# Batched 64 x 64 matmul: two rows of `a` per partition, packed 64 x 32 products, and all transfers on one queue

## The chip, the cores and the metric

The kernel runs on 1 core of one Trainium2 chip. The metric is the device time of the core in microseconds (us), the median over several executions. Each experiment was timed beside the kernel before on the same chip; that kernel's median lay between 188.4 and 189.0 us in every round, so times of different rounds are compared here as they stand. A run more than 1.5% above the fastest of its kernel is called slow; ratios below use fast runs only.

Abbreviations of the profile: PE is TensorE's matmul, PEld its weight load, DVE is VectorE, ACT is ScalarE, POOL is GpSimd, SP is SyncE. `L106` is a line of the kernel. A "group" below is 64 of the 1,024 products, the unit that the kernel loads, computes and stores; there are 16.

## The reference

```python
a = randn(1024, 64, 64)   # float32
b = randn(1024, 64, 64)   # float32
out = np.matmul(a, b)     # float32
```

The inputs are 33.5 MB together, the output 16.8 MB. The kernel computes in bf16: the loads cast from fp32 on the way.

## The kernel before

For each group, four loads on GpSimd's queue bring `a` and `b`. `a` is laid out as block diagonals of two matrices, whose zeros are written once. PE transposes each block, DVE copies the result out of PSUM, PE multiplies, and DVE and ACT each copy half of the product into `o_sb`. One store for each group goes out on SyncE's queue.

```python
a_v = a.rearrange("(g p h) r n -> g h r p n", p=P2_LG, h=2)   # runs of one row: 64 fp32 = 256 B
b_v = b.rearrange("(g s h) r n -> g h r s n", s=P2_LG, h=2)
...
for lg in range(n_lg):
    a_sb = a_tiles[lg % A_BUFS]
    for h in range(2):
        nc.gpsimd.dma_start(out=a_sb[64*h : 64*h+64, :, 64*h : 64*h+64], in_=a_v[lg, h])
    b_sb = lg_pool.tile([128, P2_LG, 64], bf16, name="b_sb")
    for s0 in range(0, P2_LG, P2_LG // 2):
        nc.gpsimd.dma_start(out=b_sb[:, s0 : s0 + P2_LG//2, :], in_=b_v[lg, :, :, s0 : s0 + P2_LG//2, :])
    o_sb = lg_pool.tile([128, LG // 4, 128], out_dt, name="o_sb")
    ...  # 4 chunks: 8 transposes of 128 x 128, copy, 16 products (K=128, M=64, N=64), 2 copies
    o_dst = out[i0 : i0 + LG].rearrange("(q b4) (t u) c -> b4 t q u c", b4=4, u=2)  # runs of 512 B
    nc.sync.dma_start(out=o_dst, in_=o_sb[:, :, :])
```

## Time and profile before

| | before |
|---|---|
| time | 188.67 us (6 runs, 188.19 to 189.46) |
| PE busy | 48% of the span |
| load packets, each writing 128 B | 131,072 |
| store packets, each 512 B | 32,768 |

From the profile page of the kernel before: PE's busy time and share, the DMA engines' busy share in 40 slices of the span (9 is 90% or more), the two queues (packets, MB, and their packets' time as a share of 16 engines' span), and the chain that ended last, by engine.

```profile
...
PE 90.0 (48%) x1536; PEld 75.9 (40%) x1536; DVE 74.4 (40%) x131; ACT 24.9 (13%) x65; POOL 72.4 (39%) x70
...
DMA  5999999999999999999999999999999999999927
...
q0 software_dynamic: 132096, 16.78, 139.5%
q1 hardware_dynamic: 33024, 16.78, 42.1%
...
DMA 68%; PE 12%; issue 7%; POOL 7%; DVE 2%; ACT 0%; POOLq 0%
```

The DMA engines are busy in every slice but the first and the last two, while PE is busy half of the time. The chain is 68% DMA. GpSimd's queue (`q0`) has a share of 139.5% because one engine has several packets under way at once, 2.45 on average from 10 to 20 us (below); such a share tells overlap, not speed.

Three stretches of the kernel before (the windows view). After the length of the stretch come busy times of the engines with their instruction counts, then the granted PE clock, the DMA share (how many packets an engine has under way on average) and the GB/s written.

```profile
...
core 0: us, PE busy (x) PEld busy (x) DVE busy (x) ACT busy (x) POOL busy (x), PEclk, DMA share, GB/s
10.00:20.00 10.00, 9.04 (x168) 7.78 (x170) 6.65 (x13) 1.61 (x5) 8.25 (x8) 1.00 2.45 156
24.00:27.50 3.50, 0.39 (x4) 0.12 (x2) 1.06 (x2) 0.00 (x0) 0.29 (x1) 0.50 1.47 213
184.00:186.00 2.00, 0.00 (x0) 0.00 (x0) 0.00 (x0) 0.00 (x0) 0.00 (x0) 0.51 1.01 290
```

The three rows are the three regimes: loads alone at 156 GB/s, loads and stores mixed at 213, stores alone at 290. Since a load writes bf16 but reads fp32, 156 GB/s written is 312 GB/s read. Divided over 16 engines, a load packet of 128 B takes 13.1 ns and a store packet of 512 B takes 28.2 ns.

What PE waited for in the kernel before (total us, times, longest):

```profile
...
PE t_ps L89 <- DMA a_diag<-in_a_dram: 60.6, 15, 10.7
...
PE o_ps L102 <- DMA b_sb<-in_b_dram: 26.4, 15, 3.9
```

PE waits for data, 60.6 + 26.4 = 87.0 us.

### The profile page before, as it was taken

How to read it: one execution, taken by the hardware profiler on the slowest of the kernel's cores; microseconds unless marked ns; L12 is line 12 of the kernel's file. 1: busy time of each engine (PE TensorE's matmuls, PEld its weight loads, DVE VectorE, ACT ScalarE, POOL GpSimd, SP SyncE). 2: the span in 40 equal slices, each digit the busy share in tenths (PEclk: the TensorE clock that was granted, in tenths of full speed). 3: DMA queues.
4: the chain of work that ended last, by engine and by line, in shares of the span. 5: the costliest groups of instructions: out<-in, count | busy, mean ns of one | idle time of the engine just before them, and what ended most of it. 6: DMA issues, size and time to landing. Idle time of an engine off the chain costs nothing.

```text
span 187.6 us, 3567 instructions
## 1 busy us (share of the span) xinstructions
PE 90.0 (48%) x1536; PEld 75.9 (40%) x1536; DVE 74.4 (40%) x131; ACT 24.9 (13%) x65; POOL 72.4 (39%) x70
## 2 busy tenths in 40 slices
PE   0079516274362913558037490575603955245840
PEld 0068415264342713546036370564503744234730
DVE  6437524135061532247124360263502545035440
ACT  2002301102011110111101120020300212002020
POOL 7997512262424514265042642336222472200000
PEclk9999955557576675576756758555855587558576
DMA  5999999999999999999999999999999999999927
GB/s 37 131 155 156 174 213 212 176 176 210 163 213 168 177 211 186 200 158 187 201 195 192 156 207 180 207 181 157 212 183 213 166 158 210 184 212 167 247 65 206
DMA packets 165136, 33.79 MB, mean 180 GB/s; under 512 B 132352, under 2 KB 165120, under 8 KB 165120
## 3 DMA queue, kind: packets, MB, share of 16 engines
q0 software_dynamic: 132096, 16.78, 139.5%
q1 hardware_dynamic: 33024, 16.78, 42.1%
q8 instruction: 12, 0.20, 0.4%
q14 instruction: 4, 0.03, 0.0%
HBM read 33.55 MB, written 16.78 MB: 268 GB/s over the span
## 4 chain that ended last, share of the span: by engine, by line
DMA 68%; PE 12%; issue 7%; POOL 7%; DVE 2%; ACT 0%; POOLq 0%
DMA b_sb<-in_b_dram 57%; DMA a_diag<-in_a_dram 11%; PE t_ps L89 8%; PE o_ps L102 5%; POOL a_diag L70 4%; POOL b_sb L77 3%; DVE a_diag L60 1%; DVE t_sb L93 0%; DVE o_sb L112 0%; ACT o_sb L113 0%; POOLq L70 0%; POOLq L77 0%
## 5 line engine op out<-in xcount | busy, mean ns | idle before, releaser
L89 PE MATMUL t_ps<-identity,a_diag 128*128 128x128 bf16 x512 | 57.6, 292 | 60.6 <-DMA a_diag<-in_a_dram 60.6
L89 PEld LDWEIGHTS <-a_diag 128*128 128x128 bf16 x512 | 46.2, 133 | 63.8 <-issue 61.8
L93 DVE COPY t_sb<-t_ps 128x1024 bf16<-128x1024 bf16 x64 | 43.6, 690 | 69.6 <-PE t_ps L89 69.3
L77 POOL DMA_DIRECT2D b_sb<-in_b_dram x32 | 37.1, 1164 | 58.3 <-issue 25.5
L102 PE MATMUL o_ps<-b_sb,t_sb 128*64 128x64 bf16 x1024 | 36.6, 231 | 30.1 <-DMA b_sb<-in_b_dram 26.4
L70 POOL DMA_DIRECT2D a_diag<-in_a_dram x32 | 34.8, 1090 | 30.1 <-DMA b_sb<-in_b_dram 21.7
L102 PEld LDWEIGHTS <-t_sb 128*64 128x64 bf16 x1024 | 29.7, 142 | 40.9 <-issue 25.5
L113 ACT COPY o_sb<-o_ps 128x256 f32<-128x256 f32 x64 | 23.7, 372 | 156.0 <-DVE o_sb L112 155.8
L112 DVE COPY o_sb<-o_ps 128x256 f32<-128x256 f32 x64 | 26.7, 423 | 35.2 <-PE o_ps L102 34.1
L60 DVE MEMSET a_diag<- 128x2048 uint32 x3 | 5.3, 1765 | 2.0 <-PEq L136 1.2
L113 ACT ACT_TABLE_LOAD x1 | 1.3, 1283 | 0.7 <-PEq L136 0.7
masks.py:199 POOL TENSOR_SCALAR_AFFINE_SELECT identity<-identity 128x128 bf16<-128x128 bf16 x1 | 0.3, 307 | 0.1
masks.py:197 POOL MEMSET identity<- 128x128 bf16 x1 | 0.2, 205 | 0.3 <-POOLq L136 0.3
L136 POOL MEMSET const-float32-0.0<- 128x1 f32 x1 | 0.1, 99 | 0.2 <-issue 0.2
L136 POOL MEMSET const-uint8-127<- 128x1 uint8 x1 | 0.1, 103 | 0.0
L136 POOL MEMSET const-bfloat16-1.0<- 128x1 bf16 x1 | 0.1, 102 | 0.0
L136 POOL MEMSET const-float32-1.0<- 128x1 f32 x1 | 0.1, 99 | 0.0
## 6 DMA issues: line engine op xcount, KB each, us to landing
out_dram<-o_sb SPq DMA_DIRECT2D x16, 1024.0 KB, 11.5
b_sb<-in_b_dram POOLq DMA_DIRECT2D x32, 256.0 KB, 18.8
a_diag<-in_a_dram POOLq DMA_DIRECT2D x32, 256.0 KB, 20.4
```

Source lines behind the costliest of these rows:

```text
L60: nc.vector.memset(a_diag, 0.0)
L70: nc.gpsimd.dma_start(out=a_sb[64 * h : 64 * h + 64, :, 64 * h : 64 * h + 64], in_=a_v[lg, h],)
L77: nc.gpsimd.dma_start(out=b_sb[:, s0 : s0 + P2_LG // 2, :], in_=b_v[lg, :, :, s0 : s0 + P2_LG // 2, :],)
L89: nc.tensor.transpose(t_ps[:, pp, :], a_sb[:, p0 + pp, :], identity)
L93: nc.vector.tensor_copy(t_sb[:], t_ps[:])
L102: nc.tensor.matmul(o_ps[orows, sigma, 64 * j : 64 * j + 64], stat[:, :, j::2], b_sb[:, p, :], start=True, stop=True,)
L112: nc.vector.tensor_copy(dst[:, :half, :], o_ps[:, :half, :])
L113: nc.scalar.copy(dst[:, half:, :], o_ps[:, half:, :])
L136: nc = _bacc.Bacc("TRN2", target_bir_lowering=False, num_devices=1)
```

## The change

It does several things at once: it reads `a` in runs of two rows (512 B); it drops the block diagonals and packs products of 64 x 32 into separate tiles of the PE array; it works in chunks of 32 products instead of 16; it issues loads two groups ahead in the program; and it moves the stores from SyncE's queue to GpSimd's. The diff, cut to its core:

```diff
-    CG = 16
+    CG = 32
-    PSUM_BUFS = 3
+    PSUM_BUFS = 2
-    a_v = a.rearrange("(g p h) r n -> g h r p n", p=P2_LG, h=2)
-    b_v = b.rearrange("(g s h) r n -> g h r s n", s=P2_LG, h=2)
+    a_v = a.rearrange("(g Qi beta) (q j) k -> g beta q Qi j k", Qi=QUADS_LG, beta=4, j=2)
+    b_v = b.rearrange("(g gamma s) r n -> g gamma r s n", gamma=2, s=LG // 2)
-    ...  # three block-diagonal tiles for a, zeroed once
+    def load(lg):
+        a_sb = lg_pool.tile([128, QUADS_LG, 128], bf16, name="a_sb")
+        nc.gpsimd.dma_start(out=a_sb[:, :, :], in_=a_v[lg])
+        b_sb = lg_pool.tile([128, 4 * SLOTS_B, 64], bf16, name="b_sb")
+        for gamma in range(2):
+            rows = slice(64 * gamma, 64 * gamma + 64)
+            nc.gpsimd.dma_start(out=b_sb[rows, :, :], in_=b_v[lg, gamma])
+        loaded[lg] = (a_sb, b_sb)
+    load(0)
+    load(1)
     for lg in range(n_lg):
+        if lg + 2 < n_lg:
+            load(lg + 2)
...      # per group: 32 transposes (64 x 128) instead of 32 (128 x 128),
...      # 128 products (K=64, M=32, N=64) instead of 64 (K=128, M=64, N=64)
-            nc.sync.dma_start(out=o_dst, in_=o_sb[:, :, :])
+        nc.gpsimd.dma_start(out=o_dst, in_=o_sb[:, :, :])
```

More of the change, by code (lines that the diff above doesn't have):

```diff
@@ L28 @@
     LG = 64 if B % 64 == 0 else B
-    CG = 16
-    STORE_BF16 = False
-    A_BUFS = 3
+    CG = 32
     SBUF_BUFS = 3
-    PSUM_BUFS = 3
+    PSUM_BUFS = 2
     assert B % LG == 0 and LG % CG == 0
@@ L37 @@
     n_cg = LG // CG
-    P2_LG = LG // 2
-    P2_CG = CG // 2
-    S4_CG = CG // 4
-    a_v = a.rearrange("(g p h) r n -> g h r p n", p=P2_LG, h=2)
-    b_v = b.rearrange("(g s h) r n -> g h r s n", s=P2_LG, h=2)
+    QUADS_LG = LG // 4
+    QUADS_CG = CG // 4
+    PAIRS_CG = CG // 8
+    SLOTS_B = LG // 8
+    assert QUADS_CG % 2 == 0, "chunk must contain whole quad pairs"
+    a_v = a.rearrange(
+        "(g Qi beta) (q j) k -> g beta q Qi j k", Qi=QUADS_LG, beta=4, j=2
+    )
+    b_v = b.rearrange("(g gamma s) r n -> g gamma r s n", gamma=2, s=LG // 2)
     consts = ctx.enter_context(tc.tile_pool(name="consts", bufs=1))
-    a_pool = ctx.enter_context(tc.tile_pool(name="a_pool", bufs=1))
     lg_pool = ctx.enter_context(tc.tile_pool(name="lg", bufs=SBUF_BUFS))
@@ L55 @@
     make_identity(nc, identity)
-    a_tiles = []
-    for ai in range(A_BUFS):
-        a_diag = a_pool.tile([128, P2_LG, 128], bf16, name=f"a_diag_{ai}")
-        nc.vector.memset(a_diag, 0.0)
-        a_tiles.append(a_diag)
-    out_dt = bf16 if STORE_BF16 else fp32
+    loaded = {}
+    def load(lg):
[6 more added lines that the diff above has]
+        loaded[lg] = (a_sb, b_sb)
@@ L65 @@
+    load(0)
+    load(1)
     for lg in range(n_lg):
         i0 = lg * LG
-        a_sb = a_tiles[lg % A_BUFS]
-        for h in range(2):
-            nc.gpsimd.dma_start(
-                out=a_sb[64 * h : 64 * h + 64, :, 64 * h : 64 * h + 64],
-                in_=a_v[lg, h],
-            )
-        b_sb = lg_pool.tile([128, P2_LG, 64], bf16, name="b_sb")
-        for s0 in range(0, P2_LG, P2_LG // 2):
-            nc.gpsimd.dma_start(
-                out=b_sb[:, s0 : s0 + P2_LG // 2, :],
-                in_=b_v[lg, :, :, s0 : s0 + P2_LG // 2, :],
-            )
@@ L82 @@
-        o_sb = lg_pool.tile([128, LG // 4, 128], out_dt, name="o_sb")
-        for cg in range(n_cg):
-            p0 = cg * P2_CG
-            t_ps = ps_pool.tile([128, P2_CG, 128], bf16, name="t_ps")
-            for pp in range(P2_CG):
-                nc.tensor.transpose(
-                    t_ps[:, pp, :], a_sb[:, p0 + pp, :], identity
-                )
-            t_sb = cg_pool.tile([128, P2_CG, 128], bf16, name="t_sb")
-            nc.vector.tensor_copy(t_sb[:], t_ps[:])
-            o_ps = ps_pool.tile([128, S4_CG, 128], fp32, name="o_ps")
-            for pp in range(P2_CG):
-                p = p0 + pp
-                sigma, colp = pp // 2, pp % 2
-                orows = slice(64 * colp, 64 * colp + 64)
-                stat = t_sb[:, pp, :].rearrange("k (hh mm) -> k hh mm", hh=2)
-                for j in range(2):
-                    nc.tensor.matmul(
-                        o_ps[orows, sigma, 64 * j : 64 * j + 64],
-                        stat[:, :, j::2],
-                        b_sb[:, p, :],
-                        start=True,
-                        stop=True,
-                    )
-            half = S4_CG // 2
-            dst = o_sb[:, cg * S4_CG : (cg + 1) * S4_CG, :]
-            nc.vector.tensor_copy(dst[:, :half, :], o_ps[:, :half, :])
-            nc.scalar.copy(dst[:, half:, :], o_ps[:, half:, :])
@@ new lines @@
+        if lg + 2 < n_lg:
+            load(lg + 2)
+        a_sb, b_sb = loaded.pop(lg)
+        o_sb = lg_pool.tile([128, QUADS_LG, 128], fp32, name="o_sb")
+        for cg in range(n_cg):
+            t_ps = ps_pool.tile([128, PAIRS_CG, 2, 128], bf16, name="t_ps")
+            for w in range(PAIRS_CG):
+                for gamma in range(2):
+                    Qi = QUADS_LG // 2 * gamma + cg * PAIRS_CG + w
+                    trows = slice(64 * gamma, 64 * gamma + 64)
+                    for j in range(2):
+                        nc.tensor.transpose(
+                            t_ps[trows, w, j, :],
+                            a_sb[:, Qi, 64 * j : 64 * j + 64],
+                            identity,
+                        )
+            t_sb = cg_pool.tile([128, PAIRS_CG, 2, 128], bf16, name="t_sb")
+            nc.vector.tensor_copy(t_sb[:], t_ps[:])
+            o_ps = ps_pool.tile([128, QUADS_CG, 128], fp32, name="o_ps")
+            for j in range(2):
+                for ql in range(QUADS_CG):
+                    w, gamma = ql // 2, ql % 2
+                    wl = cg * PAIRS_CG + w
+                    slot = (QUADS_CG // 2) * gamma + w
+                    rows = slice(64 * gamma, 64 * gamma + 64)
+                    for beta in range(4):
+                        nc.tensor.matmul(
+                            o_ps[
+                                32 * beta : 32 * beta + 32,
+                                slot,
+                                64 * j : 64 * j + 64,
+                            ],
+                            t_sb[rows, w, j, 32 * beta : 32 * beta + 32],
+                            b_sb[rows, 4 * wl + beta, :],
+                            start=True,
+                            stop=True,
+                            tile_position=(64 * gamma, 32 * beta),
+                        )
+            half = QUADS_CG // 2
+            lo = cg * PAIRS_CG
+            hi = QUADS_LG // 2 + lo
+            nc.vector.tensor_copy(o_sb[:, lo : lo + half, :], o_ps[:, :half, :])
+            nc.scalar.copy(o_sb[:, hi : hi + half, :], o_ps[:, half:, :])
@@ L115 @@
         o_dst = out[i0 : i0 + LG].rearrange(
-            "(q b4) (t u) c -> b4 t q u c", b4=4, u=2
+            "(Qi b4) (t u) c -> b4 t Qi u c", b4=4, u=2
         )
-        if STORE_BF16:
-            nc.gpsimd.dma_start(out=o_dst, in_=o_sb[:, :, :])
-        else:
-            nc.sync.dma_start(out=o_dst, in_=o_sb[:, :, :])
+        nc.gpsimd.dma_start(out=o_dst, in_=o_sb[:, :, :])
 _INS = ['a', 'b']
```

## The prediction

> **What bounds the kernel now.** The 16 DMA engines. The page's slices show DMA at 9 tenths in nearly all of the 187.6 us span, PE only 48% busy. The chain that ended last is 68% DMA, most of it `b_sb<-in_b_dram` (57%). PE waits for data (waits: `a_diag` 60.6 us, `b_sb` 26.4 us). Windows show three DMA regimes: loads alone 156 GB/s (10 to 20 us), stores alone 290 GB/s (184 to 186 us), both together 213 GB/s (24 to 27.5 us). The loads are 131,072 packets that write 128 B each (fp32 256 B read, bf16 written), the stores 32,768 packets of 512 B. Per engine, a load packet takes 128 B x 16 / 156 GB/s = 13.1 ns, a store packet 512 B x 16 / 290 GB/s = 28.2 ns. Loads alone would need 107 us, stores 58 us, together 165 us. The DMA is busy from about 3 to 187 us less a 3 us gap near 181 us, so mixing the two queues costs some 15 us more.
>
> **What the change does.** Time bought on PE, DVE or ACT is worth nothing here.
> 1. `a` is loaded in runs of two rows: 32,768 packets of 512 B read and 256 B written, instead of 65,536. `b` keeps its 65,536, the stores their 32,768. Bytes do not change. [...]
> 2. Stores move from SyncE's queue to GpSimd's, which carries the loads. Transfers then run one after another instead of interleaving. I expect most of the 15 us of mixing to go.
> 3. The diagonal zero fill (5.3 us DVE) goes; loads start no earlier.
> 4. PE: 512 transposes of half the columns, and 2,048 small matmuls instead of 1,024. At the trace's 36 ns per small matmul (16 in 0.57 us) and about 85 ns per transpose (estimate, below today's full-width 117 ns), a group of 64 products costs 7 to 8 us of PE against about 10 us of DMA. It stays hidden. DVE copies fall from 70 to about 45 us.
> 5. GpSimd still issues 64 DMAs: four per group at 1.1 us, hidden. A store waiting in this queue blocks later loads, but two groups are loaded ahead, so the DMA should not run dry.
>
> **Sum.** 53.7 (`b`) [...] + 57.8 (stores) = 157.5 us, plus 3 us before the first packet and 2 to 3 us at the end: about 163 us. Range 149 to 178. Chances: faster by over 2% 0.93, within 2% 0.04, slower 0.03.
>
> **What would show it.** DMA still at 9 tenths in all slices; about 131,000 packets, all on the software queue; [...] stores alone at about 290; no long stretch at 213. PE above 60% busy, its waits still for `a_sb` and `b_sb`.
>
> **What would make it wrong.** If a 512 B read costs two 256 B reads (26 ns), 170 us or more. If packets cost the same whatever their size, below 150 us. If software-queue stores do not take 28 ns, 10 us either way. If small matmuls cost over 50 ns, PE becomes the bound; gaps in the DMA slices would show it, as would a store that starves the loads.

The forecast's sum came to 157.5 us, and with the start and the end to about 163 us. Two terms are 4,096 x 13.1 ns for `b` and 2,048 x 28.2 ns for the stores, both from the trace before. The 85 ns for a transpose are the author's estimate; with them, products of 50 ns would make 32 x 85 + 128 x 50 ns = 9.1 us of PE for a group, beside about 10 us of DMA (estimate).

## The result, and the profile after

| | before | after |
|---|---|---|
| time | 188.79 us (16 runs, 188.19 to 189.46) | 155.04 us (8 runs, 154.93 to 155.49) |
| ratio to before | | 0.8217, 95% interval 0.8202 to 0.8233 |

A ratio is the mean time of one kernel's fast runs over that of the other's fast runs of the same rounds, so it is not quite the ratio of the medians. The kernel is 17.8% faster, inside the predicted range and 8 us below its centre.

From the profile page of the changed kernel, the same parts as above, with the count of packets and the queue that brings instructions (`q8`):

```profile
...
PE 58.6 (38%) x2560; PEld 48.4 (32%) x2560; DVE 43.4 (28%) x64; ACT 20.0 (13%) x33; POOL 72.7 (47%) x70
...
DMA  1999999999999999999999999999999999999955
...
DMA packets 103446, 33.90 MB, mean 221 GB/s; under 512 B 99328, under 2 KB 99328, under 8 KB 103424
...
q0 software_dynamic: 103424, 33.56, 171.0%
q8 instruction: 20, 0.33, 0.8%
...
issue 37%; POOL 34%; DMA 21%; PE 3%; POOLq 1%
```

The DMA engines are still busy throughout, except at the very start and end, and PE is busy even less. There are 103,446 packets, not the predicted 131,000. The missing ones are stores: 103,424 - 99,328 = 4,096 packets lie between 2 and 8 KB, and the record of single packets gives each of them 4,096 B, where SyncE's queue moved 32,768 of 512 B. So GpSimd's queue joined eight runs into one packet. "issue" in the chain is time for which the profile names no wait.

Waits of the changed kernel:

```profile
...
PE t_ps L90 <- DMA a_sb<-in_a_dram: 50.7, 15, 7.5
...
POOL out_dram L128 <- ACT o_sb L123: 21.9, 5, 8.2
...
PE o_ps L106 <- issue: 16.9, 8, 4.2
...
PE o_ps L106 <- DMA b_sb<-in_b_dram: 7.0, 14, 1.3
```

PE still waits for data, 50.7 us for `a` (60.6 before) and 7.0 us for `b` (26.4 before). Two rows are new. PE waits 16.9 us for "issue", a wait whose cause this view does not name; it matters below. And GpSimd waits 21.9 us for products before it can issue a store, with later loads standing behind that store in its queue.

The pace of the steady state is read from the chain of the changed kernel in order of time (start, length in us, what). Each row is the issue of one group's store:

```profile
...
94.39 1.17 POOL out_dram L128
...
103.23 1.17 POOL out_dram L128
...
112.39 1.17 POOL out_dram L128
...
121.67 1.17 POOL out_dram L128
...
130.98 1.17 POOL out_dram L128
```

Four groups take 130.98 - 94.39 = 36.6 us, so one takes 9.15 us, against the predicted 157.5 / 16 = 9.84 us.

PE's part of one group, from the timeline of the changed kernel (start, length, line, count, idle time before it):

```profile
...
84.75 1.92 PE L90 MATMUL t_ps<-identity,a_sb 128*64 128x128 bf16 x32 [4.32 <-DMA a_sb<-in_a_dram]
...
88.08 1.24 PE L106 MATMUL o_ps<-b_sb,t_sb 64*32 64x64 bf16 x120 [0.38 <-DMA b_sb<-in_b_dram]
```

A transpose takes 1.92 / 32 = 60 ns and a small product 1.24 / 120 = 10.3 ns.

Two windows near the end of the changed kernel, both of stores alone (columns as before):

```profile
...
core 0: us, PE busy (x) PEld busy (x) DVE busy (x) ACT busy (x) POOL busy (x), PEclk, DMA share, GB/s
142.00:146.00 4.00, 1.56 (x128) 1.20 (x124) 1.95 (x3) 1.01 (x2) 0.00 (x0) 1.00 1.00 315
149.00:152.00 3.00, 0.00 (x0) 0.00 (x0) 0.00 (x0) 0.00 (x0) 0.00 (x0) 1.00 0.99 287
```

Between these, from 146.5 to 148 us, the DMA engines have almost nothing to do (a DMA share of 0.14, 52 GB/s): the last store had to wait for the last products.

### The profile page after: what moved, and what is told of

The parts are those of the page before. It is cut to its first block, busy times and chain, and to the rows that moved or that the text cites. A ratio compares the mean times of both kernels' runs of the same rounds, so it can differ in the third digit from the quotient of the medians.

```text
span 153.7 us, 5443 instructions
## 1 busy us (share of the span) xinstructions
PE 58.6 (38%) x2560; PEld 48.4 (32%) x2560; DVE 43.4 (28%) x64; ACT 20.0 (13%) x33; POOL 72.7 (47%) x70
## 2 busy tenths in 40 slices
DMA packets 103446, 33.90 MB, mean 221 GB/s; under 512 B 99328, under 2 KB 99328, under 8 KB 103424
## 3 DMA queue, kind: packets, MB, share of 16 engines
q0 software_dynamic: 103424, 33.56, 171.0%
## 4 chain that ended last, share of the span: by engine, by line
issue 37%; POOL 34%; DMA 21%; PE 3%; POOLq 1%
DMA a_sb<-in_a_dram 21%; POOL b_sb L68 17%; POOL a_sb L63 9%; POOL out_dram L128 8%; PE t_ps L90 3%; POOLq L154 1%; POOL identity masks.py:199 0%; POOL identity masks.py:197 0%; POOLq L128 0%; POOLq L63 0%; POOLq L68 0%; POOLq masks.py:199 0%; POOLq L143 0%
## 5 line engine op out<-in xcount | busy, mean ns | idle before, releaser
L90 PE MATMUL t_ps<-identity,a_sb 128*64 128x128 bf16 x512 | 31.1, 314 | 52.9 <-DMA a_sb<-in_a_dram 50.7
L68 POOL DMA_DIRECT2D b_sb<-in_b_dram x32 | 34.9, 1095 | 28.1 <-DMA out_dram<-o_sb 21.1
L90 PEld LDWEIGHTS <-a_sb 128*64 128x64 bf16 x512 | 27.0, 173 | 55.1 <-DMA a_sb<-in_a_dram 52.6
L106 PE MATMUL o_ps<-b_sb,t_sb 64*32 64x64 bf16 x2048 | 28.5, 231 | 33.1 <-issue 16.9
L96 DVE COPY t_sb<-t_ps 128x1024 bf16<-128x1024 bf16 x32 | 22.1, 692 | 61.2 <-PE t_ps L90 61.2
L128 POOL DMA_DIRECT2D out_dram<-o_sb x16 | 18.8, 1173 | 40.4 <-ACT o_sb L123 21.9
L123 ACT COPY o_sb<-o_ps 128x512 f32<-128x512 f32 x32 | 18.8, 586 | 125.4 <-DVE o_sb L122 125.3
L106 PEld LDWEIGHTS <-t_sb 64*32 64x32 bf16 x2048 | 21.4, 101 | 41.0 <-issue 26.2
L122 DVE COPY o_sb<-o_ps 128x512 f32<-128x512 f32 x32 | 21.3, 689 | 41.0 <-PE o_ps L106 41.0
L63 POOL DMA_DIRECT2D a_sb<-in_a_dram x16 | 18.6, 1163 | 5.9 <-DMA b_sb<-in_b_dram 2.8
```

The source lines that it names most:

```text
L63: nc.gpsimd.dma_start(out=a_sb[:, :, :], in_=a_v[lg])
L68: nc.gpsimd.dma_start(out=b_sb[rows, :, :], in_=b_v[lg, gamma])
L90: nc.tensor.transpose(t_ps[trows, w, j, :], a_sb[:, Qi, 64 * j : 64 * j + 64], identity,)
L96: nc.vector.tensor_copy(t_sb[:], t_ps[:])
L106: nc.tensor.matmul(o_ps[32 * beta : 32 * beta + 32, slot, 64 * j : 64 * j + 64,], t_sb[rows, w, j, 32 * beta : 32 * beta + 32], b_sb[rows, ...
L122: nc.vector.tensor_copy(o_sb[:, lo : lo + half, :], o_ps[:, :half, :])
```

## The experiments

Four things could explain the gain: the shared queue, the larger reads of `a`, the look-ahead, and the lighter PE work. The main theory was that transfers alone set the time and that the queue brings most of it. The rivals are named in each expectation.

### 1. Undo the queue

```diff
-        nc.gpsimd.dma_start(out=o_dst, in_=o_sb[:, :, :])
+        nc.sync.dma_start(out=o_dst, in_=o_sb[:, :, :])
```

> The changed kernel with one thing undone: the stores go back to SyncE's queue, in 512 B packets, a is still read in 512 B runs. Theory (the shared queue ends the mixing of loads and stores, which cost about 15 us): 165 to 170 us, with long windows of one mixed rate, near 220 GB/s. Rival (the gain of 34 us comes from a's larger reads, or from the smaller PE work, and not from the queue): within 2% of 155 us.

Measured: 181.21 us, ratio 0.9609 to the kernel before. With the stores back on SyncE's queue, 26 of the 34 us are lost. A window of this run:

```profile
...
core 0: us, PE busy (x) PEld busy (x) DVE busy (x) ACT busy (x) POOL busy (x), PEclk, DMA share, GB/s
60.00:63.00 3.00, 0.29 (x8) 0.17 (x9) 0.69 (x1) 0.00 (x0) 1.09 (x1) 1.00 1.45 213
```

The mixed regime of 213 GB/s is back. The rival (`a`'s reads or PE bring the whole gain) is refuted. This run keeps the loads two groups ahead, so it shows what the queue is worth beside the look-ahead. The theory's size was also too small: the loss was larger than the 10 to 15 us expected.

### 2. Undo the larger reads of `a`

```diff
-        nc.gpsimd.dma_start(out=a_sb[:, :, :], in_=a_v[lg])
+        for j in range(2):
+            nc.gpsimd.dma_start(
+                out=a_sb[:, :, 64 * j : 64 * j + 64],
+                in_=a_v[lg].rearrange("beta q Qi j k -> j beta q Qi k")[j],
+            )
```

> The changed kernel with one thing undone: each a load is split in two, one per row of the pair, so that every packet reads 256 B and writes 128 B again; stores stay on GpSimd's queue. Theory (a 512 B read takes about 20 to 22 ns against 13.1 ns for 256 B): 2,048 x (26.2 - 21) ns, so 10 to 13 us more, 165 to 168 us. Rival A (cost goes with bytes): 155 to 157 us. Rival B (cost goes with packets): 27 us more, about 180 us.

Measured: 163.58 us, ratio 0.8674, so 8.5 us more than the changed kernel. That is a little less than expected and between both rivals. It includes the cost of one more transfer for each group (five instead of four).

### 3. The transfers by themselves

```diff
-    ...  # loads, products, copies, stores of every group
+    for lg in range(8): load_a512(lg)                # 1: a in 512 B reads
+    for lg in range(8, 16): load_a256(lg)            # 2: a in 256 B reads
+    for lg in range(8): load_b(lg)                   # 3: b in 256 B reads
+    for lg in range(5): store(nc.gpsimd, lg)         # 4: stores, GpSimd's queue
+    nc.vector.memset(o_sb, 2.0)                      # waits for 4
+    for lg in range(5, 10): store(nc.sync, lg)       # 5: stores, SyncE's queue
+    nc.vector.memset(o_sb, 3.0)                      # waits for 5
+    for lg in range(10, 16): store(nc.sync, lg)      # 6: both queues
+    for i in range(4): load_b(8 + i, l_sb[i])
```

> No product is computed, the result is wrong on purpose. Six phases one after another: a in 512 B reads, a in 256 B reads, b in 256 B reads, stores on GpSimd's queue, stores on SyncE's queue, then stores on SyncE's beside loads of b on GpSimd's. Expected from the traces: a at 512 B 200 GB/s (20 to 22 ns a packet), a and b at 256 B both 156 GB/s, stores on SyncE's queue 290 GB/s. Stores on GpSimd's queue: 290 GB/s if only the mixing matters; clearly more, 315 GB/s or above, if the 4 KB packets of that queue are cheaper by themselves. Mixed phase: 213 GB/s, less than the two rates in turn allow (with one packet of each in turn, 640 B in 41.3 ns per engine is 248 GB/s).

The result is wrong, as meant; it is a single run, so its state is unknown. The scheduler started the last loads earlier than written, behind phase 4, so that they met the stores of phase 5; phase 6 then ran stores alone. The windows, in order: `a` at 512 B, loads at 256 B, stores on GpSimd's queue (two rows), both queues mixed, stores on SyncE's queue alone.

```profile
...
core 0: us, DVE busy (x) POOL busy (x), PEclk, DMA share, GB/s
16.00:25.00 9.00, 0.00 (x0) 3.42 (x3) 1.00 1.83 182
32.00:78.00 46.00, 0.00 (x0) 30.51 (x28) 1.00 2.45 156
82.00:86.00 4.00, 0.00 (x0) 1.92 (x2) 1.00 1.02 384
88.00:95.00 7.00, 0.00 (x0) 2.05 (x2) 1.00 1.00 274
110.00:118.00 8.00, 0.00 (x0) 0.00 (x0) 1.00 1.47 212
141.00:160.00 19.00, 0.00 (x0) 0.00 (x0) 1.00 1.01 284
```

A 512 B read of `a` writes 256 B at 182 GB/s, which is 256 x 16 / 182 = 22.5 ns; the trace of the changed kernel has the same rate, 183 GB/s from 17.5 to 19 us. The 20 to 22 ns of the expectations, the author's estimate, were a little low. Loads of 256 B keep 156 GB/s, and mixing gives 212. New is the store on GpSimd's queue: 384 GB/s over the first 2 MB, or 21.3 ns for 512 B, against 284 GB/s on SyncE's queue. But in a longer run of stores it fell to 274 GB/s. The changed kernel stores 1 MB at a time with loads between. Why the rate falls is open; in the changed kernel too the last store, alone, moved only 287 GB/s. So the higher rate was seen only in the first 2 MB of this run of stores: later, and in that last store, GpSimd's large packets moved 274 to 287 GB/s, no more than SyncE's small ones did alone (284 here, 290 in the kernel before).

### 4. The two changes of order alone

The kernel before keeps its block diagonals, its products and its 256 B reads.

```diff
-        nc.sync.dma_start(out=o_dst, in_=o_sb[:, :, :])
+        nc.gpsimd.dma_start(out=o_dst, in_=o_sb[:, :, :])
 ...
+    load(0)
+    load(1)
     for lg in range(n_lg):
+        if lg + 2 < n_lg:
+            load(lg + 2)
```

> The kernel before, its products and its 256 B reads of a kept, with the two changes of order alone: loads issued two groups ahead and stores on GpSimd's queue. Theory (the transfers alone set the time, the PE work is hidden): the same as the run with a in 256 B pieces within 2%, 165 to 168 us. Rival (the smaller matmul and copy work matters too): clearly slower than that run, by over 4 us.

Measured: 161.63 us, ratio 0.858. It is even 2 us faster than the run of section 2, which has lighter PE work and the same five transfers for each group. So the rival falls: the lighter PE and DVE work bought nothing visible. Together with section 1 this gives a table of two by two (medians):

| | stores on SyncE's queue | stores on GpSimd's queue, loads ahead |
|---|---|---|
| `a` in 256 B reads | 188.85 (before) | 161.63 |
| `a` in 512 B reads | 181.21 | 155.04 (after) |

From left to right the time falls by 26 to 27 us in either row, from top to bottom by 6.6 to 7.6 us in either column. The table is not clean: of the left column only the run of 181.21 us has the look-ahead, and the lower row also has the new products. So in the upper row the 27 us are queue and look-ahead together; what the look-ahead does beside stores on SyncE's queue was not tested.

### 5. Stores on GpSimd's queue in small packets

```diff
-        o_sb = lg_pool.tile([128, QUADS_LG, 128], fp32, name="o_sb")
+        o_sb = lg_pool.tile([128, QUADS_LG, 128], bf16, name="o_sb")
```

> The changed kernel with the output tile in bf16, so that the store casts on its way (as the loads do, which the profile counts as one packet for each run). Stores stay on GpSimd's queue, nothing mixes. Theory P (the software queue's gain over the prediction comes from its 4 KB packets): the stores become 32,768 packets of 512 B, about 28 ns each as on SyncE's queue, and the time about 163 us, what the prediction had. Rival Q (one queue is all that matters, whatever the packet): 155 us within 2%. The result is a little less exact, which is meant.

Measured: 157.91 us, ratio 0.8351. The packets were small, as meant:

```profile
...
DMA packets 132117, 33.89 MB, mean 217 GB/s; under 512 B 99328, under 2 KB 132096, under 8 KB 132096
```

But the time rose by only 2.9 us, not 8, so the joined packets are about a third of what the prediction missed, if all of that rise is theirs. The windows in the middle of two stores show how the small packets kept up:

```profile
...
60.00:61.00 1.00, 0.59 (x56) 0.46 (x57) 0.00 (x0) 0.00 (x0) 0.49 (x2) 1.00 2.99 374
69.00:70.00 1.00, 0.42 (x36) 0.29 (x37) 0.20 (x1) 0.00 (x0) 1.00 (x2) 1.00 2.96 363
```

A DMA share of 2.96 to 2.99 means that each engine had three of these packets under way. On SyncE's queue it was 1.01 (section 3): one packet at a time. The run isn't a clean one-factor test, since the store now reads half the bytes from the core's own memory.

### 6. Stores on SyncE's queue in large packets

```diff
-            "(Qi b4) (t u) c -> b4 t Qi u c", b4=4, u=2
+            "p (h r) c -> p h (r c)", h=2
         )
-        nc.gpsimd.dma_start(out=o_dst, in_=o_sb[:, :, :])
+        nc.sync.dma_start(out=o_dst, in_=o_sb[:, :, :])
```

> The changed kernel with stores on SyncE's queue but in runs of 8 KB in HBM instead of 512 B: the rows land in wrong places on purpose. Theory P (small store packets are slow, and they interleave with load packets one by one): with large packets 155 to 160 us although two queues are used. Rival R (two queues side by side lose time by themselves): 175 to 182 us, as with 512 B stores on SyncE's queue.

Measured: 152.55 us, ratio 0.8055, and a wrong result, as meant. SyncE's queue now moved the same bytes in 2,304 packets (2,048 of data):

```profile
...
q1 hardware_dynamic: 2304, 16.78, 27.5%
```

A window of one store in this run:

```profile
...
61.00:63.00 2.00, 0.24 (x4) 0.11 (x5) 0.35 (x1) 0.00 (x0) 0.70 (x1) 1.00 1.08 402
```

This refutes that a second queue costs time by itself: with 8 KB packets it runs at 402 GB/s and the kernel is as fast as any here. What was slow is a store in 512 B packets on SyncE's queue. Three durations fit one line: 28.2 ns for 512 B (SyncE), 4,096 x 16 / 384 = 171 ns for 4 KB (GpSimd, section 3), and 8,192 x 16 / 402 = 326 ns for 8 KB (SyncE). The first and last give about 8 ns for each packet and 20 ns for each 512 B (estimate), and 167 ns for 4 KB, near the 171 measured. That agrees with a cost of about 8 ns for each packet where an engine has one under way at a time. It holds for the fast part of section 3 only: at the 274 GB/s of the longer run a 4 KB packet takes 4,096 x 16 / 274 = 239 ns, far off the line. Mixing costs something beside that: one packet of each in turn would give 640 B in 41.3 ns, or 248 GB/s on 16 engines, and 213 were measured.

### 7. The transfers of the changed kernel without products

```diff
-        for cg in range(n_cg): ...   # transposes, products, copies
+        nc.vector.tensor_copy(o_sb[:, 0, 0:64], a_sb[:, 0, 0:64])
+        nc.vector.tensor_copy(o_sb[0:64, 0, 64:128], b_sb[0:64, 0, :])
+        nc.vector.tensor_copy(o_sb[64:128, 0, 64:128], b_sb[64:128, 0, :])
```

> The changed kernel's transfers, order and buffers, but no transposes, products or evictions (wrong on purpose; one small copy for each load keeps the wait for it). Theory (the transfers alone set the time, PE and the queue order cost only the start and the end): 148 to 154 us. Rival (products delay stores and so loads): under 145 us.

Measured: 152.2 us, ratio 0.8045, as the theory had it. The whole of PE's, ACT's and nearly all of DVE's work is worth 3 us. The changed kernel is bound by its transfers.

### 8. Larger reads of `b` too

If `a` gains from 512 B reads, `b` should. It then lies with two rows on a partition, so each product becomes two accumulated halves of 32 rows, and PE gets 640 instructions for a group instead of 320.

```diff
-    b_v = b.rearrange("(g gamma s) r n -> g gamma r s n", gamma=2, s=LG // 2)
+    b_v = b.rearrange("(G g s) (q j) n -> G g q s j n", g=4, s=LG // 4, j=2)
 ...
-        tile_position=(64 * gamma, 32 * beta),
+        tile_position=(32 * g, 32 * beta),      # twice, start=(jk == 0), stop=(jk == 1)
```

> A further step: b too is read in runs of 512 B, two rows on a partition, and the product runs as two accumulated halves of 32 rows each. Theory (a load of 512 B takes 22.5 ns against 13.1 ns for 256 B, and the transfers alone set the time): saves 2,048 x (26.2 - 22.5) ns = 7.6 us, so 147 to 149 us. Rival (PE work, which grows to about 7 us for a group, or the four b transfers for a group on GpSimd's queue, now bind): 153 us or more. The result should be correct.

Measured: 233.13 us, ratio 1.2275, correct and far slower than either theory. The profile's DMA row and instruction queue, then two waits:

```profile
...
DMA  5999990799909996399917999099980899923606
...
q8 instruction: 39, 0.64, 1.2%
```

```profile
...
POOL out_dram L126 <- ACT o_sb L121: 135.9, 16, 15.1
...
PEld L110 <- issue: 97.6, 41, 7.7
```

DMA now has holes. PE's weight loads wait 97.6 us for "issue", the products come late, GpSimd waits 135.9 us to issue stores, and the loads stand behind them. The instruction queue moved 0.64 MB in 39 packets of 16 KB, where the changed kernel moved 0.33 MB in 20: one packet for 256 of its 5,120 PE instructions (2,560 matmuls and as many weight loads). In the record of instructions, PE's gaps began after these counts of PE instructions:

```
changed kernel with b in 512 B:  449  705  961  1217  1729  1985  2241  2497 ...
differences:                         256  256  256   512   256   256   256
```

The gaps lie 256 instructions apart, or two blocks. The packets of the instruction queue stand in the record of the core's DMA engines, and their times settle what "issue" is here: each of the 32 waits of PE's matmuls for "issue" over 1 us in this run ended 1.2 to 1.7 us after one of these packets had landed. The same holds for all 7 in the changed kernel (1.3 to 1.6 us) and all 28 in the run of section 9; the kernel before had no such wait. So PE waited for its next block of 256 instructions, which comes as a DMA packet beside the data.

### 9. More PE instructions, same transfers

Section 8 changed other things too, so this run changes only the number of PE instructions.

```diff
-                    for beta in range(4):
+                    for beta in [0, 1, 2, 3, 0, 1, 2, 3]:
                         nc.tensor.matmul(
```

> The changed kernel with every small matmul issued twice, into the same place with the same operands: transfers, order and result unchanged, PE instructions 320 to 576 for each group of 64. It tells apart why the run with b in 512 B was slow. Theory F (the PE's instructions arrive in blocks of 256, each by a transfer that waits among the data; in that run a block took about 5.8 us, and PE's gaps lay 256 instructions apart): 16 x 2.25 x 5.8 us, about 200 to 215 us. Rival G (the doubled matmuls cost array time only, 128 x 10 ns a group, which is hidden; the slow run was slow for its four small b transfers or its 32-row tiles): within 3% of 155 us.

Measured: 227.72 us, median of 222.29 to 228.3. Its runs scatter by 2.7%, so only the fastest, 222.29, counts as fast, and no interval exists; that one is 18% above the 189.0 us of the kernel before and 43% above the changed kernel. Theory F holds in its mechanism and G falls; the time lies above the 200 to 215 us that F expected. The doubled products cost 128 x 10.3 ns = 1.3 us of array time for a group; the delay for a group was over 4 us. The profile of one of the slower runs, with its DMA row and instruction queue:

```profile
...
DMA  5999994993999999992999959999599998980606
...
q8 instruction: 35, 0.57, 0.9%
```

PE in its timeline:

```profile
...
61.06 0.49 PE L106 MATMUL o_ps<-b_sb,t_sb 64*32 64x64 bf16 x34 [5.41 <-issue]
61.48 1.92 PE L90 MATMUL t_ps<-identity,a_sb 128*64 128x128 bf16 x32
...
67.45 1.36 PE L106 MATMUL o_ps<-b_sb,t_sb 64*32 64x64 bf16 x128 [2.56 <-issue]
```

Blocks of 128 products, which are 256 instructions with their weight loads, stand between waits for "issue" of 2.6 to 5.4 us. 16 x 576 / 256 = 36 blocks in 226 us are about 6.3 us for each (estimate). The changed kernel needs 1.25 blocks for a group, which at this pace would be about 7.9 us of its 9.15 (estimate). By that it was close to this bound. Its 16.9 us of "issue" waits are the same thing (section 8), still hidden. What sets the pace of the blocks is open.

### 10. Take the look-ahead out

```diff
-    load(0)
-    load(1)
     for lg in range(n_lg):
-        if lg + 2 < n_lg:
-            load(lg + 2)
+        load(lg)
```

> The changed kernel with the explicit early loads taken out: each group's load stands at the head of its own turn. The instruction order on GpSimd shows that the scheduler still moves loads ahead of stores, but fewer of them. Theory (a store that waits in the shared queue holds back the loads behind it, so loads must be issued two groups ahead): 160 to 175 us. Rival (the scheduler's own lookahead and the three buffers suffice): within 1% of 155 us.

Measured: 179.27 us (median of all four runs), ratio 0.9472 (three fast runs, 178.54 to 179.65). The look-ahead is worth 24 us, more than expected, and the shared queue is of little use without it: SyncE's queue with the look-ahead took 181.21 us (section 1). This wait is from a profile of its one slow run, 181.67 us:

```profile
...
POOL out_dram L125 <- ACT o_sb L120: 100.2, 16, 10.2
```

GpSimd waits 100.2 us in 16 stores, against 21.9 us in 5 in the changed kernel. In its timeline GpSimd issues nothing from 69.7 us until a store at 79.5 us, and the next loads right behind that store.

### 11. Load `b` without a cast

```diff
-        b_sb = lg_pool.tile([128, 4 * SLOTS_B, 64], bf16, name="b_sb")
+        b_sb = lg_pool.tile([128, 4 * SLOTS_B, 64], fp32, name="b_f32")
 ...
+            nc.scalar.copy(b_sb[:, part, :], b_f32[:, part, :])
```

> The changed kernel with b loaded as fp32, without a cast on the way, on GpSimd's queue, and cast to bf16 by ScalarE, which is 87% idle. Theory (without a cast this queue joins short runs into 4 KB packets, as it does for the stores, at about 170 ns for 4 KB, 10.7 ns for 256 B instead of 13.1): the b packets fall from 65,536 to 4,096 and the time to about 145 to 147 us. Rival (a load of 256 B runs costs the same in any packet, or more because 256 B are written instead of 128 B): 155 us or more.

Measured: 186.43 us, ratio 0.9845. Half of the theory held: the packets were joined, and 41,984 are left on the queue.

```profile
...
q0 software_dynamic: 41984, 41.95, 117.1%
```

The other half failed. A window in which `b` was loaded (PE got its `a` at 68.0 us, ScalarE its `b` at 73.6 us):

```profile
...
68.00:72.00 4.00, 1.70 (x26) 1.46 (x27) 0.69 (x1) 0.00 (x0) 1.79 (x2) 0.50 0.99 189
```

They read at about 189 GB/s, while the cast loads of 256 B read 312. Joining runs into 4 KB packets paid for stores of 512 B runs and cost for loads of 256 B runs. The reason is open: the run also writes twice the bytes into the core's memory.

### 12. `a` in runs of 1 KB

Four rows on a partition, with no more PE instructions. The copy out of PSUM sorts rows so that products and stores stay as they were.

```diff
-    a_v = a.rearrange("(g Qi beta) (q j) k -> g beta q Qi j k", Qi=QUADS_LG, beta=4, j=2)
+    a_v = a.rearrange("(g o b) (q j) k -> g b q o j k", o=LG // 8, b=8, j=4)
 ...
-            nc.vector.tensor_copy(t_sb[:], t_ps[:])
+            nc.vector.tensor_copy(t_sb[:].rearrange("k w h bq jj -> k w h jj bq"), t_ps[:])
```

> A further step with no more PE instructions: a is read in runs of 1 KB, four rows on a partition, and the copy out of PSUM sorts the rows so that the products and the stores stay as they are. Theory (a load packet costs 13.1 ns for 256 B and 22.5 ns for 512 B, so 9.4 ns for each 256 B more, 41 ns for 1 KB; the transfers alone set the time): 1,024 x (45.0 - 41.3) ns, 3.8 us less, about 151 us, faster than both kernels. Rival (larger reads gain nothing more, or the longer copy delays the products): 155 us or more. The result should be correct.

Measured: 152.27 us, ratio 0.8078 (0.8049 to 0.8106), correct. Packets fell again:

```profile
...
DMA packets 87062, 33.90 MB, mean 225 GB/s; under 512 B 66560, under 2 KB 82944, under 8 KB 87040
```

This is the fastest correct kernel here, ahead of the changed one (0.8217, intervals apart), though by 2.8 us and not the 3.8 expected.

## Why the prediction was right or wrong, point by point

- **The bound: right.** The prediction said that only DMA counts. Without any products the transfers take 152.2 us of 155.04 (section 7), and the old PE work with the new order is no slower (section 4).
- **Point 1, the reads of `a`: right, but its size was not worked out from this case.** The figure it gave is cut. Measured: a packet that reads 512 B takes 22.5 ns, two that read 256 B take 2 x 13.1 = 26.2 ns. That makes 2,048 x 3.7 ns = 7.6 us (estimate), and the runs show 6.6 to 8.5 us. The figure of a load is not that of a store: 512 B on SyncE's queue took 28.2 ns.
- **Point 2, the queue: right in direction, too small.** "Most of the 15 us of mixing" was predicted; the queue brings 26 to 27 us. In the changed kernel the transfers did run largely one after another: 157 GB/s with a DMA share of 2.45 from 20 to 22 us, as in loads alone, and 379 GB/s with 1.14 from 32 to 34 us, near the store rate of section 3. The step that failed is the term "57.8 (stores)", carried over from SyncE's queue. In the steady state a group takes 9.15 us. `a` takes 0.524 MB / 182 GB/s = 2.88 us of it and `b` 0.524 / 156 = 3.36. The remaining 2.91 us are the store, about 360 GB/s or 46.6 us in all (estimate; 16 packets of 171 ns on each engine would be 2.74 us). This is 11 us less than predicted. With the 15 us of mixing that the prediction named, it makes the 26 us of section 1; the two parts were not measured apart. The packet count of 131,000 was wrong with it.
- **Point 3, the zero fill: right.** The first load packet started 3.3 us into the span before and after.
- **Start and end: too small.** Predicted 5.5 us; 155.04 - 16 x 9.15 = 8.6 us. Together: -11 and +3 make the 8 us by which the centre was off, so one error hid part of the other.
- **Why stores are cheaper there: partly settled.** Joined packets alone don't explain it, since small ones cost only 2.9 us more (section 5). Nor is a second queue slow by itself (section 6). The runs agree with a cost of about 8 ns for each packet where only one is under way, but nothing shows that mechanism directly, and the fall to 274 GB/s in long runs of stores stays open. There 4 KB packets were no faster than single ones of 512 B on SyncE's queue.
- **Point 4, PE: hidden, as said, but with wrong figures.** PE is 38% busy, not over 60%; a small product takes 10.3 ns, not 36, and a transpose 60, not 85. And the danger was named wrongly: not array time but the delivery of instructions. PE's matmuls grew from 1,536 to 2,560, each with its weight load, and by the estimate of section 9 about 7.9 of 9.15 us went to their delivery. The prediction did not have this term at all: that PE stayed hidden was luck, and by that estimate by a narrow margin.
- **Point 5, the look-ahead: right.** Without it the stores starve the loads: GpSimd waited 100.2 us in its stores and the kernel took 24 us more (section 10).

## What to carry to other kernels

In a kernel bound by DMA, work out the time of one packet in each regime of the trace (each direction, each queue, and mixed) and don't carry a figure from one queue to another: 512 B of a store took 28 ns on one and about 23 on the other (estimate), with loads between the stores. If stores share the loads' in-order queue, issue the loads far enough ahead, or the store that waits for its data stops them (24 us here). Before replacing few large matmuls by many small ones, count PE instructions in blocks of 256 and compare the blocks' arrival, here about 6 us each beside the data transfers, with the time that the group has.
